# A hybrid attention and recurrence layer on one core: earlier weight splits, a two-pass rotary key, attention's output weights prepared one stage earlier, rotated queries written twice

## The chip, the core and the metric

The kernel runs on one core of a Trainium2 chip as one program. The metric is the device time of one execution in microseconds; smaller is better. The kernel before took 829.15 us (median of three runs, 826.8 to 831.96).

## What is computed

One layer over 1024 tokens of 1024 features, all in float32, cut to what matters here:

```python
h    = rms_norm(x, norm1_g) * (1 + scale1) + shift1      # mod = silu(c) @ w_ada + b_ada
proj = h @ w_in                  # 256 q latents, 128 kv latents, 64 rotary key, 512 x_lru, 512 g_lru
q    = rms_norm(q_lat) @ w_q_b   # 4 heads of 128 + 64 rotary
kv   = rms_norm(kv_lat) @ w_kv_b # 4 heads of 128 key + 128 value
attn = causal_softmax_attention(rope(q), rope(k), v)
lru  = scan(a, b) * gelu(g_lru)  # a, b from two sigmoid gates on a width-4 convolution of x_lru
mixed = concat([rms_norm(attn), rms_norm(lru)])          # 512 + 512
x    = x + gate1 * (mixed @ w_out)
h2   = rms_norm(x, norm2_g) * (1 + scale2) + shift2
x    = x + gate2 * experts(h2)   # 4 groups of 8 experts, top group, top 2 experts of it
```

## The kernel before

**Precision.** A float32 operand is cut into a high and a low part of a shorter format, and a product is made of three matmuls: high by high, high by low, low by high (`mm3`, L224 to L227). `split` (L216 to L222) makes the parts: a copy on ScalarE (ACT) writes the high part (L218, or L221 with a scale), and a subtraction writes the low one, on VectorE (DVE) or GpSimd (POOL) (L219, or L222 with a scale).

**Memory.** Most operands live in one pool of 41 blocks of 128 x 1024 floats (`blk`). A tile takes the block that is next in the ring, and waits until the readers of its last tenant are done. Transfers from memory stand in the queue of SyncE (SP): a load that waits for a block holds up the loads behind it. PSUM accumulators come from named banks: `pp` (projections) and `pL` (the recurrent branch's output) share three banks.

**Order.** The code is written as generators that are interleaved; a scheduler then fixes each engine's own instruction order at build time. Each engine runs its list strictly in order.

**Stages**, with the times of the trace:

- 0 to 180 us: twelve projections of the normalized input, one after the other in a list `FT`: kv latents, two of q latents, four of x_lru (`xl`), the rotary key (`kr`, index 7, 64 columns), and from index 8 four of g_lru (`gl0` to `gl3`). Between them stand the recurrence's gates (`gate_mm`, sigmoid; `gate`, exponentials, a square root L581, the scan L586) and the streamed modulation product (`wad`, L486 and L490). Projection i loads the weights of i+2 (`load_in`) and splits those of i+1 (`split_in`, L266).
- 180 to 233: the last gate, then `gl0` to `gl3` (`gl_steps`, L997) merged with head 0's keys and values (`pkv`). Each `gl` result goes through gelu, a product with the scan's output, and a square that POOL adds into `sqL` (L650).
- 233 to 246: head 0's queries (`pq`, L806). The rotary part of a pair of query tiles is formed by L521 to L524 on DVE and copied to a second place by POOL (L819).
- 246 to 297: `l_pass` (L1043), the recurrent branch's half of `mixed @ w_out`: 16 groups of 12 matmuls into `pL`, two groups to each of eight tiles of x (`xr`), which are stored back to `x_d`. Its weights come from `out_w([4, 5, 6, 7])` (L1017): four loads `wo`, 16 products with gate1 on POOL (L1027), and four scaled splits into `woh` and `wol` (L221, L222). The branch's norms (`pc`, L1040) need the finished `sqL`.
- 297 to 410: heads 0 to 2 (scores `pS`, probabilities `P`, transposed `PT`, values `po`), each merged with the preparation of the next one.
- 410 to 510: head 3 merged with attention's half of the output projection, whose weights come from `out_w([0, 1, 2, 3])`, stepped inside head 3.
- 510 to 545: router and lists; then to 825 the experts, with weights `ew` streamed by SP (L1101).

Of the kernel before, what the change touches and what calls it, by code (L numbers as in the profile page):

```python
# [22 lines left out]
NT = 8  # L23
# [115 lines left out]
def layer(ctx, tc, A, out, dbg=None, stop=None):  # L139
# [10 lines left out]
    def blk(name, dt=F32):  # L150
        return big.tile([128, 1024], dt, name=name, tag="b", bufs=NBLK)
# [64 lines left out]
    def split(src, hi, lo, scale=None, eng=None):  # L216
        if scale is None:
            SC.activation(hi, src, AF.Copy)  # L218
            (eng or V).tensor_sub(lo, src, hi)  # L219
        else:  # L220
            SC.activation(hi, src, AF.Copy, scale=scale)  # L221
            V.scalar_tensor_tensor(lo, src, scale, hi, op0=OP.mult, op1=OP.subtract)  # L222
# [6 lines left out]
    def t3(ap, t):  # L229
        return ap.rearrange("p (t f) -> p t f", t=t)  # L230
# [35 lines left out]
    def split_in(i):  # L266
        if i >= len(FT):
            return
        M = 64 if FT[i][0] == "kr" else 128
        w = wraw.pop(i)  # L270
        wh, wl = (t3(blk(n, F32R), 8)[:, :, :M] for n in ("winh", "winl"))
        split(w, wh, wl, eng=EN[OPT["in_lo" if i >= OPT["k1"] else "in_l1"]])
        wsp[i] = (wh, wl)

    pin = ctx.enter_context(ExitStack())
    pin.enter_context(ordered(*(EN[e] for e in OPT["pin"])))
# [247 lines left out]
        V.tensor_add(dst, dst, tmp)  # L524

    def project(i, n, ks=range(8)):
        M = 64 if FT[i][0] == "kr" else 128
        wh, wl = wsp[i]
        if 0 in ks:
            hold[i] = bank("pp")  # L530
        pp = hold[i]
        for k in ks:
            mm3(pp[:M], wh[:, k], wl[:, k], hTh[k][:, NS[n]], hTl[k][:, NS[n]], k == 0, k == 7)
            if k % 4 == 3:
                yield

# [87 lines left out]
    def k_rope(i, n):  # L624
        pp = hold.pop(i)
        if n == 0:
            lq["kr"] = blk("krT")
        kr = lq["kr"]
        SC.activation(kr[:64, NS[n]], pp[:64], AF.Copy)
        if n == 1:  # L630
            pk = bank("pk")
            for t in range(NT):
                T.transpose(pk[:, t * 64:(t + 1) * 64], kr[:64, t * 128:(t + 1) * 128], ident[:64, :64])
            kb = blk("kb")
            sqr, tmp = t3(kb[:, :512], NT), t3(kb[:, 512:], NT)
            SC.activation(sqr, t3(pk, NT), AF.Square)
            V.tensor_reduce(ssr, sqr, op=OP.add, axis=AX.X)
            rope(krr, t3(pk, NT), NT, "k", 0, tmp)

# [85 lines left out]
    for i in range(8):  # L725
        kind, j = FT[i]
        if i >= K1:
            load_in(i + 2)
            split_in(i + 1)
        if kind == "xl":  # L730
            load_gate(j)
        for n in range(2) if i >= K1 else (1,):
            for _ in project(i, n) if i >= K1 else ():
                for _ in range(OPT["adv"]):
                    next(ag, None)
            if n == (0 if i >= K1 else 1):
                gates()
            evac(i, n)
        if i < K1:
            wsp.pop(i)  # L740
        if i == 1:
            split_in(K1)
            V.tensor_scalar(rst, rsti, 0, None, op0=OP.is_equal)
            V.tensor_scalar(rcap, rst, -1.0, 2.0, op0=OP.mult, op1=OP.add)
        if kind == "xl":
            pend.append(j)
    wk = blk("wk")
    wq = [blk("wq")[:, :768] for _ in range(2)]
    SY.dma_start(wk, A["w_kv_b"])
    with tc.issue_after(last["x"]):  # L750
        for k in range(2):
            SY.dma_start(wq[k], A["w_q_b"][k * 128:(k + 1) * 128, :])
    gates(True)
    wkh, wkl = blk("wkh", F32R), blk("wkl", F32R)
    split(wk, wkh, wkl, eng=EN[OPT["wk_lo"]])
    drain(ag)
    sqL = blk("sqL")
    SCALE = 192.0 ** -0.5
# [3 lines left out]
    def prep(h, P):  # L762
# [39 lines left out]
        def q_mm(t0):  # L802
            pq = t3(bank("pq"), 2)[:, :, :192]
            for a in range(2):
                for k in range(2):
                    T.matmul(pq[:, a], latq[k][:, (t0 + a) * 128:(t0 + a) * 128 + 128], wq[k][:, h * 192:(h + 1) * 192],  # L806
                             start=(k == 0), stop=(k == 1))
            qnp = half("qnp").rearrange("p (c a d) -> p c a d", c=2, a=2)
            qn, qp = qnp[:, 0], qnp[:, 1]
            SC.activation(qn, pq[:, :, :128], AF.Copy)  # L810
            sqh = sm.tile([128, 2, 192], F32, name="sqh2", bufs=1)
            if OPT["ssh"]:
                for a in range(2):
                    SC.activation(sqh[:, a], pq[:, a], AF.Square, accum_out=ssh[:, t0 + a:t0 + a + 1])
            else:
                SC.activation(sqh, pq, AF.Square)
            tm = sm.tile([128, 2, 64], F32, name="qtmp", bufs=1)
            rope(qp[:, :, :64], pq[:, :, 128:], 2, "q", t0, tm)
            G.tensor_copy(qp[:, :, 64:], qp[:, :, :64])  # L819
            if not OPT["ssh"]:  # L820
                V.tensor_reduce(ssh[:, t0:t0 + 2], sqh, op=OP.add, axis=AX.X)
            qst[t0] = qn, qp
# [174 lines left out]
    def gl_steps():  # L997
        for i in range(8, 12):
            load_in(i + 2)
            split_in(i + 1)  # L1000
            for n in range(2):
                yield from project(i, n)
                evac(i, n)
                yield


# [36 lines left out]
    def l_pass():  # L1043
        mod_row("g1", 2)
        yield from out_w([4, 5, 6, 7])
        norms(ivL, sqL, list(range(NT)))
        for g in range(4):
            gs = slice(g * 256, g * 256 + 256)
            mh, ml = blk("mLh", F32R), blk("mLl", F32R)
            for j in range(4):  # L1050
                split(lru[j][:, gs], mh[:, j * 256:j * 256 + 256], ml[:, j * 256:j * 256 + 256], eng=EN[OPT["mL"]])
            for t in (2 * g, 2 * g + 1):
                x = blk("xr")
                SY.dma_start(x, A["x"][t * 128:(t + 1) * 128, :])
                for n in range(2):
                    pL = bank("pL")
                    for f in range(4):
                        c = slice(f * 256 + (t % 2) * 128, f * 256 + (t % 2) * 128 + 128)
                        mm3(pL, mh[:, c], ml[:, c], woh[4 + f][:, NS[n]], wol[4 + f][:, NS[n]], f == 0, f == 3)
                    V.scalar_tensor_tensor(x[:, NS[n]], pL, ivL[:, t:t + 1], x[:, NS[n]], op0=OP.mult, op1=OP.add)  # L1060
                    yield
                SY.dma_start(x1_d[t * 128:(t + 1) * 128, :], x)

# [75 lines left out]
    for h in range(3):  # L1139
# [1 line left out]
        ahead(30 + h)  # L1141
        merge((attention(h, P), OPT["mg"]), (prep(h + 1, Pn), NPREP))
        P = Pn
    ow = out_w([0, 1, 2, 3])
    next(ow)
    ahead(33)


# [239 lines left out]
    for i in attention(3, P, after):  # L1388
        if i is not None:
            ahead(20 + i)  # L1390
            next(ow, None)
            if i == OPT["rw"]:
                router_w()
            if i >= OPT["hk"]:
                next(ws_)
    drain(ow)
    if OPT["sep"]:
        phase(2)
    drain(ws_)
# [355 lines left out]
```

## Time and profile before

| what | value |
|---|---|
| median of three runs | 829.15 us (826.8 to 831.96) |
| the profiled execution | 831.86 us |
| its span in the trace | 830.1 us (1.76 us lie around it) |
| granted TensorE clock, mean | 0.956 |
| busy: PE / DVE / ACT / POOL | 736.3 / 449.1 / 316.9 / 163.5 us |

PE is TensorE's matmuls, PEld its weight loads, which overlap them. The profiled execution is 2.7 us above the median. A share of busy time is a mean over all stages; what a change is worth is read stage by stage: windows (busy time of each engine in a stretch), the timeline (instructions in order, with the idle time before each and what ended it) and the waits.

### The profile page before, as it was taken

To read this page: it belongs to the slowest core of one execution; us is meant where nothing else is said; L and a number is where in the kernel's file an instruction comes from. 1 tells how busy PE (TensorE), PEld (TensorE's weight loads), DVE (VectorE), ACT (ScalarE), POOL (GpSimd) and SP (SyncE) were. 2 spreads that over 40 slices of the span, in tenths; PEclk is the share of its full clock that TensorE was granted. 3 is DMA by queue.
4 is the path that set the end of the run, shared out by engine and by line. 5 is a ranking of instruction groups with operands and counts; after the bars stand their busy time and mean duration, and the time that the engine had idled before them with its cause. 6 is when DMAs were issued, how large, how long until landed. Compare 5 with 4: busy or idle time off the path is not lost. (4 is left out here: it accounts for less than half of the span.)

```text
span 830.1 us, 12292 instructions
## 1 busy us (share of the span) xinstructions
PE 736.3 (89%) x4265; PEld 475.6 (57%) x4265; DVE 449.1 (54%) x1332; ACT 316.9 (38%) x715; POOL 163.5 (20%) x167
## 2 busy tenths in 40 slices
PE   3799999996989989898979998599987799999985
PEld 1387766465878878788868887333333234333231
DVE  4597296886658359787985567343442122221311
ACT  3455555764444047667754444021111112120210
POOL 1111002122580002032631100111221111221101
PEclk9989999996989999999989999699988999999998
DMA  9942447681214340202144779999999999999993
GB/s 313 374 132 83 140 140 239 209 255 51 77 51 181 123 152 2 64 14 102 41 145 152 257 255 343 369 320 312 322 358 333 330 367 340 330 370 334 333 309 71
DMA packets 70976, 180.47 MB, mean 217 GB/s; under 512 B 8960, under 2 KB 22528, under 8 KB 70912
## 3 DMA queue, kind: packets, MB, share of 16 engines
q1 hardware_dynamic: 63328, 158.50, 53.9%
q0 software_dynamic: 7104, 21.00, 9.6%
q8 instruction: 34, 0.56, 0.3%
q10 hardware_dynamic: 480, 0.16, 0.2%
q14 instruction: 30, 0.25, 0.1%
HBM read 160.61 MB, written 22.95 MB: 221 GB/s over the span
## 5 line engine op out<-in xcount | busy, mean ns | idle before, releaser
L1629 PE MATMUL pgu<-ew,xeT 128*32 128x512 f32 (+1 forms) x928 | 165.3, 616 | 12.9 <-DMA ew<-in_w_e 11.6
L1629 PEld LDWEIGHTS pgu<-ew,xeT 128*32 128x32 f32 (+1 forms) x928 | 47.4, 122 | 104.6 <-issue 80.8
L225 PE MATMUL pp<-hTh,winh 128*128 128x512 f32 (+1 forms) x192 | 76.0, 408 | 5.1 <-DVE hTh L188 3.0
L1640 PE MATMUL py<-ew,hT 128*32 128x512 f32 (+1 forms) x464 | 78.4, 603 | 2.2 <-ACT hT L1614 2.2
L227 PE MATMUL pp<-hTh,winl 128*128 128x512 f32 (+1 forms) x192 | 77.2, 402 | 0.9 <-DVE winl L219 0.9
L226 PE MATMUL pp<-hTl,winh 128*128 128x512 f32 (+1 forms) x192 | 77.7, 405 | 0.0
L1643 DVE TENSOR_TENSOR y<-py,m_g 128x512 f32<-128x512 f32 (+1 forms) x40 | 27.7, 691 | 79.0 <-PE py L1640 74.2
L1603 ACT ACTIVATE sg<-pgu 128x256 f32<-128x256 f32 (+1 forms) x20 | 7.7, 387 | 133.0 <-PE pgu L1629 133.0
L1640 PEld LDWEIGHTS py<-ew,hT 128*32 128x32 f32 (+1 forms) x464 | 24.6, 121 | 47.1 <-issue 38.5
L1645 POOL DMA_INDIRECT out<-y,pki x13 | 20.7, 1596 | 134.2 <-DVE y L1643 118.3
L1596 DVE TENSOR_SCALAR xeT<-pxe,gc,mc 128x128 f32<-128x128 f32 x80 | 27.3, 403 | 35.1 <-PE pxe L1590 33.8
L225 PEld LDWEIGHTS pp<-hTh,winh 128*128 128x128 f32 (+1 forms) x192 | 36.5, 190 | 16.9 <-DVE hTh L188 3.9
L1614 ACT ACTIVATE hT<-pht 128x256 f32<-128x256 f32 (+1 forms) x20 | 7.6, 381 | 96.8 <-PE pht L1612 92.6
L1605 DVE SCALAR_TENSOR_TENSOR hid<-sg,pkw,pgu 128x256 f32<-128x256 f32 (+1 forms) x13 | 6.2, 478 | 69.4 <-ACT sg L1603 69.4
L227 PEld LDWEIGHTS pp<-hTh,winl 128*128 128x128 f32 (+1 forms) x192 | 36.2, 189 | 12.1 <-issue 2.5
L226 PEld LDWEIGHTS pp<-hTl,winh 128*128 128x128 f32 (+1 forms) x192 | 36.4, 189 | 11.6 <-issue 2.1
L1594 ACT ACTIVATE xeT<-pxe,mc,gc 128x128 f32<-128x128 f32 x80 | 30.0, 461 | 26.0 <-PE pxe L1590 26.0
L965 PE MATMUL po<-PT,v 128*128 128x256 f32 (+1 forms) x160 | 36.3, 366 | 0.0
L931 ACT ACTIVATE P<-pS,nb,scq 128x384 f32<-128x384 f32 (+2 forms) x48 | 32.4, 684 | 10.1 <-DVE nb L928 9.7
L965 PEld LDWEIGHTS po<-PT,v 128*128 128x128 f32 x160 | 29.3, 194 | 3.0
L806 PE MATMUL pq<-wq,latq 128*128 128x192 f32 x128 | 25.4, 352 | 5.7 <-DVE v L782 3.4
L1590 PEld LDWEIGHTS pxe<-ident,xe 128*128 128x128 f32 x160 | 18.5, 145 | 19.3 <-issue 12.3
(419 smaller groups left out, 1612.0 us busy)
## 6 DMA issues: line engine op xcount, KB each, us to landing
ew<-in_w_e SPq DMA_DIRECT2D x186, 512.0 KB
wad<-in_w_ada SPq DMA_DIRECT2D x64, 256.0 KB
wada<-in_w_ada SPq DMA_DIRECT2D x16, 512.0 KB
win<-in_w_in SPq DMA_DIRECT2D x12, 512.0 KB
xt<-in_x SPq DMA_DIRECT2D x8, 512.0 KB
wo<-in_w_out SPq DMA_DIRECT2D x8, 512.0 KB
xr<-in_x SPq DMA_DIRECT2D x8, 512.0 KB
x_d<-xr SPq DMA_DIRECT2D x8, 512.0 KB
```

The lines of the kernel that those rows point to most:

```text
L225: T.matmul(o, lhi, rhi, start=first, stop=False)
L226: T.matmul(o, lhi, rlo, start=False, stop=False)
L227: T.matmul(o, llo, rhi, start=False, stop=last)
L806: T.matmul(pq[:, a], latq[k][:, (t0 + a) * 128:(t0 + a) * 128 + 128], wq[k][:, h * 192:(h + 1) * 192], start=(k == 0), stop=(k == 1))
L931: SC.activation(Pt[:, o:o + w], pss[ci], AF.Exp, scale=P["scq"][:, i:i + 1], bias=nb, accum_out=l[:, ci:ci + 1])
L965: T.matmul(po[:, o:], P["v"][:, js], PT[j // 4][:, j % 4, o:], start=(j == 0), stop=(j == nj - 1), skip_group_check=True)
L1594: SC.activation(xT[a][:, c], pt[:, c], AF.Identity, scale=gc[:, k:k + 1], bias=sh2[:, k:k + 1])
L1596: last["dve"] = V.tensor_scalar(xT[a][:, c], pt[:, c], gc[:, k:k + 1], sh2[:, k:k + 1], op0=OP.mult, op1=OP.add).ins
L1629: T.matmul(pg[r], xT[k // 4][:, c + r.start:c + r.stop], w[k // 2][:, NS[k % 2]], start=(k == 0), stop=(k == 7), skip_group_check=True)
L1640: T.matmul(py[n][r], hT[:, a * 128 + r.start:a * 128 + r.stop], w[4 + a][:, NS[n]], start=(a == 0), stop=(a == 1), skip_group_check=True)
L1643: last["dve"] = V.tensor_mul(y[:rows, NS[n]], py[n][:rows], mrow["g2"][:rows, NS[n]]).ins
L1645: G.indirect_dma_start(out=out, out_offset=bass.IndirectOffsetOnAxis(ap=idx, axis=0), in_=y[r0:r0 + idx.shape[0]], in_offset=None, compute ...
```

## The change

Four edits. **One**: the rotary key's weights, high and low, stand in one block side by side (64 and 64 columns), so that two passes (against the high and the low input) give both parts in 128 rows instead of three passes with 64; the eight transposes that follow become eight matmuls against a stacked identity, which add the two halves. **Two**: the weights of `gl1` and of `w_kv_b` are split before the last gate, the latter's low part on DVE instead of POOL; each later `gl` is split two ahead, after the first half of a projection. **Three**: `out_w([0, 1, 2, 3])` is stepped inside `l_pass` instead of head 3: loads at its second quarter (`g == 1`), products and splits in the third and fourth. **Four**: the last addition of the rotated query writes both places, and POOL's copy goes.

```diff
--- before.py
+++ after.py
@@ -266,11 +266,15 @@
     def split_in(i):
         if i >= len(FT):
             return
-        M = 64 if FT[i][0] == "kr" else 128
         w = wraw.pop(i)
-        wh, wl = (t3(blk(n, F32R), 8)[:, :, :M] for n in ("winh", "winl"))
-        split(w, wh, wl, eng=EN[OPT["in_lo" if i >= OPT["k1"] else "in_l1"]])
-        wsp[i] = (wh, wl)
+        if FT[i][0] == "kr":
+            wb = t3(blk("winh", F32R), 8)
+            wh, wl = wb[:, :, :64], wb[:, :, 64:]
+            wsp[i] = (wb, None)
+        else:
+            wh, wl = wsp[i] = tuple(t3(blk(n, F32R), 8) for n in ("winh", "winl"))
+        last["hi"] = SC.activation(wh, w, AF.Copy).ins
+        last["lo"] = EN[OPT["in_lo" if i >= OPT["k1"] else "in_l1"]].tensor_sub(wl, w, wh).ins
 
     pin = ctx.enter_context(ExitStack())
     pin.enter_context(ordered(*(EN[e] for e in OPT["pin"])))
@@ -524,13 +528,16 @@
         V.tensor_add(dst, dst, tmp)
 
     def project(i, n, ks=range(8)):
-        M = 64 if FT[i][0] == "kr" else 128
         wh, wl = wsp[i]
         if 0 in ks:
             hold[i] = bank("pp")
         pp = hold[i]
         for k in ks:
-            mm3(pp[:M], wh[:, k], wl[:, k], hTh[k][:, NS[n]], hTl[k][:, NS[n]], k == 0, k == 7)
+            if wl is None:
+                T.matmul(pp, wh[:, k], hTh[k][:, NS[n]], start=(k == 0), stop=False)
+                T.matmul(pp, wh[:, k], hTl[k][:, NS[n]], start=False, stop=(k == 7))
+            else:
+                mm3(pp, wh[:, k], wl[:, k], hTh[k][:, NS[n]], hTl[k][:, NS[n]], k == 0, k == 7)
             if k % 4 == 3:
                 yield
 
@@ -626,14 +633,17 @@
         if n == 0:
             lq["kr"] = blk("krT")
         kr = lq["kr"]
-        SC.activation(kr[:64, NS[n]], pp[:64], AF.Copy)
+        SC.activation(kr[:, NS[n]], pp, AF.Copy)
         if n == 1:
+            i2 = half("ident2")[:, :64]
+            V.tensor_add(i2, ident[:, :64], ident[:, 64:])
             pk = bank("pk")
             for t in range(NT):
-                T.transpose(pk[:, t * 64:(t + 1) * 64], kr[:64, t * 128:(t + 1) * 128], ident[:64, :64])
+                T.matmul(pk[:, t * 64:(t + 1) * 64], kr[:, t * 128:(t + 1) * 128], i2, start=True, stop=True)
             kb = blk("kb")
             sqr, tmp = t3(kb[:, :512], NT), t3(kb[:, 512:], NT)
-            SC.activation(sqr, t3(pk, NT), AF.Square)
+            with tc.issue_after(last["hi"]):
+                SC.activation(sqr, t3(pk, NT), AF.Square)
             V.tensor_reduce(ssr, sqr, op=OP.add, axis=AX.X)
             rope(krr, t3(pk, NT), NT, "k", 0, tmp)
 
@@ -727,6 +737,8 @@
         if i >= K1:
             load_in(i + 2)
             split_in(i + 1)
+            if i == 7:
+                split_in(i + 2)
         if kind == "xl":
             load_gate(j)
         for n in range(2) if i >= K1 else (1,):
@@ -735,6 +747,12 @@
                     next(ag, None)
             if n == (0 if i >= K1 else 1):
                 gates()
+            if (i, n) == (7, 1):
+                wk = blk("wk")
+                SY.dma_start(wk, A["w_kv_b"])
+                wkh, wkl = blk("wkh", F32R), blk("wkl", F32R)
+                last["hi"] = SC.activation(wkh, wk, AF.Copy).ins
+                V.tensor_sub(wkl, wk, wkh)
             evac(i, n)
         if i < K1:
             wsp.pop(i)
@@ -744,15 +762,11 @@
             V.tensor_scalar(rcap, rst, -1.0, 2.0, op0=OP.mult, op1=OP.add)
         if kind == "xl":
             pend.append(j)
-    wk = blk("wk")
     wq = [blk("wq")[:, :768] for _ in range(2)]
-    SY.dma_start(wk, A["w_kv_b"])
     with tc.issue_after(last["x"]):
         for k in range(2):
             SY.dma_start(wq[k], A["w_q_b"][k * 128:(k + 1) * 128, :])
     gates(True)
-    wkh, wkl = blk("wkh", F32R), blk("wkl", F32R)
-    split(wk, wkh, wkl, eng=EN[OPT["wk_lo"]])
     drain(ag)
     sqL = blk("sqL")
     SCALE = 192.0 ** -0.5
@@ -815,8 +829,12 @@
             else:
                 SC.activation(sqh, pq, AF.Square)
             tm = sm.tile([128, 2, 64], F32, name="qtmp", bufs=1)
-            rope(qp[:, :, :64], pq[:, :, 128:], 2, "q", t0, tm)
-            G.tensor_copy(qp[:, :, 64:], qp[:, :, :64])
+            a_, b_ = tabs["q"]
+            V.tensor_mul(qp[:, :, 64:], pq[:, :, 128:], a_[:, t0:t0 + 2])
+            V.tensor_mul(tm[:, :, 0:32], pq[:, :, 160:], b_[:, t0:t0 + 2, 0:32])
+            V.tensor_mul(tm[:, :, 32:], pq[:, :, 128:160], b_[:, t0:t0 + 2, 32:])
+            two_ = lambda v: v[:, :, None, :].to_broadcast([128, 2, 2, 64])
+            V.tensor_add(qp.rearrange("p a (r d) -> p a r d", r=2), two_(qp[:, :, 64:]), two_(tm))
             if not OPT["ssh"]:
                 V.tensor_reduce(ssh[:, t0:t0 + 2], sqh, op=OP.add, axis=AX.X)
             qst[t0] = qn, qp
@@ -997,10 +1015,11 @@
     def gl_steps():
         for i in range(8, 12):
             load_in(i + 2)
-            split_in(i + 1)
             for n in range(2):
                 yield from project(i, n)
                 evac(i, n)
+                if n == 0:
+                    split_in(i + 2)
                 yield
 
 
@@ -1044,7 +1063,10 @@
         mod_row("g1", 2)
         yield from out_w([4, 5, 6, 7])
         norms(ivL, sqL, list(range(NT)))
+        ow = out_w([0, 1, 2, 3])
         for g in range(4):
+            if g == 1:
+                next(ow)
             gs = slice(g * 256, g * 256 + 256)
             mh, ml = blk("mLh", F32R), blk("mLl", F32R)
             for j in range(4):
@@ -1058,6 +1080,8 @@
                         c = slice(f * 256 + (t % 2) * 128, f * 256 + (t % 2) * 128 + 128)
                         mm3(pL, mh[:, c], ml[:, c], woh[4 + f][:, NS[n]], wol[4 + f][:, NS[n]], f == 0, f == 3)
                     V.scalar_tensor_tensor(x[:, NS[n]], pL, ivL[:, t:t + 1], x[:, NS[n]], op0=OP.mult, op1=OP.add)
+                    if g > 1:
+                        next(ow, None)
                     yield
                 SY.dma_start(x1_d[t * 128:(t + 1) * 128, :], x)
 
@@ -1141,8 +1165,6 @@
         ahead(30 + h)
         merge((attention(h, P), OPT["mg"]), (prep(h + 1, Pn), NPREP))
         P = Pn
-    ow = out_w([0, 1, 2, 3])
-    next(ow)
     ahead(33)
 
 
@@ -1388,12 +1410,10 @@
     for i in attention(3, P, after):
         if i is not None:
             ahead(20 + i)
-            next(ow, None)
             if i == OPT["rw"]:
                 router_w()
             if i >= OPT["hk"]:
                 next(ws_)
-    drain(ow)
     if OPT["sep"]:
         phase(2)
     drain(ws_)
```

**ACT at the last gate.** The rows are ACT's from the projection of the rotary key to the first gelu results; `winh` is the high part of a projection's weights, `wkh` that of `w_kv_b`, `kb` the square of the rotary key, `sqL` the square of the first gelu product; L581 (now L588) is the square root of a gate. Before:

```order
L218 ACTIVATE winh<-win 128x1024
L581 ACT_TABLE_LOAD
L581 ACTIVATE gt_wa<-gt_wa 128x1024
L564 ACT_TABLE_LOAD
...
L581 ACT_TABLE_LOAD
L581 ACTIVATE gt_wa<-gt_wa 128x1024
L636 ACTIVATE kb<-pk 128x512
L644 ACT_TABLE_LOAD
L644 ACTIVATE gelu<-pp 128x512 x2
L218 ACTIVATE wkh<-wk 128x1024
L218 ACTIVATE winh<-win 128x1024
L647 ACTIVATE sqL<-gt_wa 128x512 x2
```

With the change:

```order
L276 ACTIVATE winh<-win 128x1024 x2
L588 ACT_TABLE_LOAD
L588 ACTIVATE gt_wa<-gt_wa 128x1024
L571 ACT_TABLE_LOAD
...
L754 ACTIVATE wkh<-wk 128x1024
L588 ACT_TABLE_LOAD
L588 ACTIVATE gt_wa<-gt_wa 128x1024
L646 ACTIVATE kb<-pk 128x512
L654 ACT_TABLE_LOAD
L654 ACTIVATE gelu<-pp 128x512 x3
L657 ACTIVATE sqL<-gt_wa 128x512 x2
L276 ACTIVATE winh<-win 128x1024
```

The high part of `gl1` has moved ahead of the third gate's square root, `wkh` ahead of the last one's; the next high part (`gl2`) stands behind three gelus and two squares.

**POOL around the second output weights.** The rows are POOL's; `wo<-wo,m_g` is the product with gate1, four for each weight block, `sqA` belongs to head 3's results. Before, in head 2's end and head 3:

```order
L830 MEMSET ql 64x512
L1402 MEMSET xe 128x1024
L819 COPY qnp<-qnp 128x2x64
L976 TENSOR_TENSOR sqA<-sqA,sqa 128x256
L1027 TENSOR_TENSOR wo<-wo,m_g_1955 128x256 x16
L976 TENSOR_TENSOR sqA<-sqA,sqa 128x256 x4
```

With the change, in `l_pass`:

```order
L660 TENSOR_TENSOR sqL<-sqL,gelu 128x512
L848 MEMSET ql 64x512
L1046 TENSOR_TENSOR wo<-wo,m_g_1940 128x256 x16
L848 MEMSET ql 64x512
L807 TENSOR_TENSOR kraw<-kraw,ik 128x1024
L810 TENSOR_TENSOR sqh<-krr,ik 128x8x64 x2
```

The 16 products now stand ahead of the next head's key products (`kraw`, `sqh`), and no copy L819 is left.

**SP in l_pass.** The rows are SP's transfers, from the first output weights on. Before:

```order
L1021 DMA wo<-in_w_out 128x1024 x4
L1054 DMA xr<-in_x 128x1024 x2
L1062 DMA x_d<-xr 128x1024 x2
L1054 DMA xr<-in_x 128x1024 x6
L1062 DMA x_d<-xr 128x1024 x6
L1101 DMA ew<-in_w_e 128x1024 x7
L1021 DMA wo<-in_w_out 128x1024 x4
```

With the change:

```order
L1040 DMA wo<-in_w_out 128x1024 x4
L1076 DMA xr<-in_x 128x1024 x2
L1086 DMA x_d<-xr 128x1024
L1040 DMA wo<-in_w_out 128x1024
L1086 DMA x_d<-xr 128x1024
L1040 DMA wo<-in_w_out 128x1024 x3
L1076 DMA xr<-in_x 128x1024 x4
L1086 DMA x_d<-xr 128x1024 x2
L1076 DMA xr<-in_x 128x1024 x2
```

The second four weight loads, seven rows behind the first ones in the list of before, now stand between the second tile of x and the third.

## Rows read from the trace of the kernel before

**Rows 1.** The page: the span in 40 slices, DMA engines' busy tenths and GB/s.

```profile
DMA  9942447681214340202144779999999999999993
GB/s 313 374 132 83 140 140 239 209 255 51 77 51 181 123 152 2 64 14 102 41 145 152 257 255 343 369 320 312 322 358 333 330 367 340 330 370 334 333 309 71
```

**Rows 2.** Windows: stretch, length, busy PE, PEld, DVE, ACT, POOL, clock, DMA, GB/s.

```profile
180.00:200.00 20.00, 12.87 (x52) 9.80 (x51) 17.81 (x20) 9.55 (x12) 8.12 (x7) 0.67 0.21 61
330.00:340.00 10.00, 8.38 (x58) 7.57 (x57) 6.34 (x23) 4.78 (x14) 0.00 (x0) 1.00 0.00 1
410.00:420.00 10.00, 5.36 (x31) 4.24 (x29) 9.83 (x17) 4.34 (x10) 10.00 (x12) 0.95 0.17 52
420.00:430.00 10.00, 9.22 (x51) 8.79 (x52) 8.09 (x17) 6.92 (x15) 1.76 (x3) 0.71 0.32 112
```

**Rows 3.** Waits of SP's queue: us in total, times, longest.

```profile
SPq L1101 <- DMA ew<-in_w_e: 185.5, 144, 4.5
```

**Rows 4.** Timeline of PE at the last gate: start, us, instruction, idle before and releaser.

```profile
185.39 0.71 PE L633 MATMUL pk<-ident,krT 64*128 64x64 f32 x8
190.13 0.79 PE L225 MATMUL pkv<-wkh,latkh 128*128 128x256 f32 x2 [4.03 <-ACT wkh L218]
191.08 0.80 PE L225 MATMUL pp<-hTh,winh 128*128 128x512 f32 x1 [0.15 <-ACT winh L218]
...
195.22 0.58 PE L226 MATMUL pkv<-wkl,latkh 128*128 128x256 f32 x1 [2.06 <-POOL wkl L219]
...
196.90 0.80 PE L227 MATMUL pp<-hTh,winl 128*128 128x512 f32 x1 [0.89 <-DVE winl L219]
...
200.48 0.45 PE L226 MATMUL pp<-hTl,winh 128*128 128x512 f32 x1
```

**Rows 5.** The same in the last projections: first and last of 93 matmuls.

```profile
211.84 0.40 PE L225 MATMUL pp<-hTh,winh 128*128 128x512 f32 x1
...
232.73 0.39 PE L227 MATMUL pp<-hTh,winl 128*128 128x512 f32 x1
```

**Rows 6.** Timelines of SP, PE and ACT ahead of the third gate.

```profile
163.08 0.43 SPq L254 DMA_DIRECT2D win<-in_w_in  x1
...
167.75 1.06 PE L490 MATMUL pm<-wad,cs 128*32 128x512 f32 x8 [1.16 <-DMA wad<-in_w_ada]
...
163.81 1.04 ACT L218 ACTIVATE winh<-win 128x1024 fp32r<-128x1024 f32 x1
```

**Rows 7.** Timeline of POOL from the third addition to `sqL` to the last.

```profile
218.96 1.29 POOL L650 TENSOR_TENSOR sqL<-sqL,gelu 128x512 f32<-128x512 f32 x1 [4.66 <-ACT gelu L649]
...
228.36 8.50 POOL L1027 TENSOR_TENSOR wo<-wo,m_g 128x256 f32<-128x256 f32 x10
...
243.68 1.43 POOL L650 TENSOR_TENSOR sqL<-sqL,gelu 128x512 f32<-128x512 f32 x1
```

**Rows 8.** Timeline of PE at the start of `l_pass`.

```profile
246.06 0.48 PE L225 MATMUL pL<-woh,mLh 128*128 128x512 f32 x1
```

**Rows 9.** Timeline of DVE in `l_pass`: one of nine, 2.72 us apart.

```profile
278.87 0.75 DVE L1060 SCALAR_TENSOR_TENSOR xr<-pL,ivL,xr 128x512 f32<-128x512 f32 x1 [1.97 <-PE pL L227]
```

**Rows 10.** Timeline of POOL in head 3; durations of line L222 (min/median/max ns).

```profile
407.01 13.34 POOL L1027 TENSOR_TENSOR wo<-wo,m_g 128x256 f32<-128x256 f32 x16
...
L222 DVE SCALAR_TENSOR_TENSOR wol<-wo,col,woh x8: 1273/1285/2247, 224.2 to 424.6; 128x1024 fp32r<-128x1024 f32 x8
```

**Rows 11.** Timeline of DVE: the same scaling during POOL's products, and in head 0.

```profile
411.79 0.87 DVE L945 TENSOR_SCALAR P<-P,rl 128x128 f32<-128x128 f32 x1
...
300.60 0.28 DVE L945 TENSOR_SCALAR P<-P,rl 128x128 f32<-128x128 f32 x1
```

**Rows 12.** Durations of two lines on DVE (min/median/max ns).

```profile
L524 DVE TENSOR_TENSOR qnp<-qnp,qtmp x16: 275/292/855, 240.2 to 402.8; 128x128 f32<-128x128 f32 x16
...
L219 DVE TENSOR_TENSOR mLl<-gt_wa,mLh x16: 405/417/1481, 243.5 to 266.0; 128x256 fp32r<-128x256 f32 x16
```

**Rows 13.** Waits from 300 to 420 us: us in total, times, longest.

```profile
PE ptP L952 <- ACT P L931: 2.5, 2, 1.6
```

## The prediction

> **What bounds the kernel now.** I read the page's slices first, then windows by stage, then the timelines at the holes. Two regimes show. From about 540 us on the DMA engines are busy nine tenths or more of every slice but the last, at 309 to 370 GB/s [rows 1], and SP waited 144 times, 185.5 us in all, for an earlier load of expert weights [rows 3]: there the stream of weights sets the pace. Its loads wait for blocks that the stages ahead give back, so the stream begins earlier when those stages end earlier. Before that TensorE is the limiter wherever it is full, and time is lost only where it is not. In the windows [rows 2] it is idle 7.1 of 20 us at 180 to 200, at a granted clock of 0.67; 4.6 of 10 us at 410 to 420; and at 420 to 430 it is busy 9.22 us at a clock of 0.71. An ordinary head (330 to 340) has 8.38 of 10 at full clock. The change touches the first two of these places and puts work into l_pass, which is nearly full. So the sum is three stretches of PE's timeline, and every microsecond saved ahead of 430 is taken to move all that follows.
>
> **Part two, the last gate.** PE's transposes end at 186.10 (185.39 + 0.71), and at 200.48 it is back at full pace [rows 4]. In these 14.4 us it does 12 matmuls of 512 columns and 4 of 256. At full clock 93 of the long ones took 232.73 − 211.84 = 20.89 us, 0.227 us apiece [rows 5]; a short one half of it. The work is worth 12 × 0.227 + 4 × 0.114 = 3.2 us, so 11.2 us are lost: 4.03 us waiting for wkh, 2.06 for wkl, 0.89 for the low part of gl0 [rows 4], the rest on half a clock (0.67 in the window, with matmuls 0.43 us apart between 197.5 and 200.1) after these stalls. All three operands are now made earlier: wkh ahead of the last gate's square root, wkl on DVE, both parts of gl1 before the gate. What is late next? First, ACT's queue: gl1's high part (1.04 us [rows 6]) now stands ahead of the third gate's square root, and it needs the load issued at 163.08, which shares the DMA engines with modulation pieces, for which PE waited until 167.75 [rows 6]. I estimate that load to land at 168 to 169.5, against 164.85 when ACT ended the high part ahead (163.81 + 1.04), so the gates' chain on ACT and DVE slips 3 to 4.5 us. Second, gl2's high part now stands behind three gelus and two squares, which wait for the scan; PE has 24 matmuls of gl1 (5.4 us) and head 0's pkv to cover that, and runs dry for 1 to 3 us. Bounds: 11.2 if nothing is late, 3.7 if both slips land whole on PE (11.2 − 4.5 − 3). I take 8, in the upper half since the matmuls of gl0 and gl1 are there to run while the gate finishes.
>
> **Part one, the rotary key.** 48 matmuls become 32: 16 × 0.227 = 3.6 us of PE [rows 5]. Matmuls on 64 and on 128 columns of weights move 512 columns either way, so the price is the count. The unmoved waits of that stretch (convolution output for the gates, the modulation piece at 167.75 [rows 6]) give part of it back: between 0 and 3.6 I take 1.5, below half, because the next event there is a load. The eight plain matmuls in place of transposes (0.71 us for all eight [rows 4]) and one addition on DVE: under 1 us either way, hidden beside the scan, at nothing; without that cover it is 1 us.
>
> **The chain to l_pass.** POOL is busy without a break from the third addition to sqL at 218.96 to the end of the last at 243.68 + 1.43 = 245.11, and the first pL matmul is at 246.06 [rows 7, 8]: ten products alone take 8.50 us. This chain starts on a gelu result, so it moves with parts one and two; two copies leave it (0.3 to 0.9 us each by the DVE twin of their size [rows 12]; at least 0.6): +0.5. l_pass then starts 8 + 1.5 + 0.5 = 10 us earlier, at 236 (bounds 3.7 and 11.2 + 3.6 + 0.5 = 15.3).
>
> **Part three, what it puts into l_pass.** 16 products on POOL, 13.34 us in head 3 [rows 10]; four scaled low parts on DVE, 1.285 us each [rows 10], 5.1 in all, with as many high parts on ACT; four loads of 512 KB. POOL and ACT have little to do there. DVE takes 0.75 us of each 2.72 us group and idles 1.97 [rows 9]: over 16 groups 31 us are free, so 5.1 fit, with the products' own disturbance too. Queued behind: three weight loads now stand ahead of the third tile of x in SP's list. 1.57 MB at 374 GB/s, the page's best slice [rows 1], are 4.2 us. The tile's reader is the addition that frees a pL bank; three banks are two groups ahead, so that some of the 4.2 us is covered. PE waits 0 (all covered) to 4.2 us; a gain is excluded, since nothing leaves this stage but copies. I take 1.5.
>
> The same edit in head 3: at 410 to 430 PE lost 4.64 us by idling, then 0.78 and 9.22 × 0.29 = 2.67 by the clock: 8.1 us [rows 2]. An ordinary head loses 1.62 in 10, 3.2 in 20. Gain 8.1 − 3.2 = 4.9, taken as 5; bounds 3 (the router's weights and head 3's start remain in DVE's list) and 8.1. Here a scaling of 128 x 128 took DVE 0.87 us beside POOL's products against 0.28 in head 0 [rows 11], so these products slow DVE, and through it the softmax, well beyond their own count.
>
> The Trainium skill, "SBUF — State Buffer", section "SBUF: two separate sides", says that DVE and GpSimd take turns on one shared port pair, held for a whole instruction, the loser blocked. By that rule the 13.34 us would stop DVE wherever they stand, l_pass included; by the rows there is room for them, and the sum keeps 1.5 us.
>
> **Part four.** The second copy makes DVE's addition 256 wide: 0.417 against 0.292 us [rows 12], 16 × 0.125 = 2.0 us over four heads, beside PE's work; 16 POOL copies and a hop DVE to POOL go. Taken at nothing; without the cover −2.0, and up to +1 at head 0's queries.
>
> **Sum.** 10 − 1.5 + 5 = 13.5 us. The profiled execution took 831.86 (span 830.1 and 1.76 around it): 818.4 for it. It stands 2.7 above the median 829.15, so the prediction is 829.15 − 13.5 = 815.65. All bad ends at once give 3.7 − 4.2 + 3 − 2 = 0.5, all good ones 15.3 + 8.1 + 1 = 24.4; without either pile-up the forecast's own range is a gain of 6 to 22, 807 to 823.
>
> **Rivals.**
> - *The hole only moves.* ACT stands before the third gate's square root for gl1's load, the gate ends so late that gl2 waits, and POOL's chain sets l_pass. For: the load stands among modulation pieces that PE itself waits for [rows 6]. Against: 11.2 us were lost to operands that are now early. Front gain 2: 829.15 − 2 + 1.5 − 5 = 823.7.
> - *The products' price is paid again in l_pass.* DVE, blocked 13.34 us, delays the additions that free pL; two spare groups (5.4 us) cover part, 8 us remain: 829.15 − 10 − 5 + 8 = 822. It is the shared-port rule named above, at work on this kernel. Against: DVE idles 1.97 of 2.72 us [rows 9].
> - *The stream of weights ends the kernel anyway.* 144 waits on it [rows 3]; if its start did not follow the stages ahead, 829. Against: the middle slices of the page move 2 to 181 GB/s [rows 1], so it is blocks, not the DMA engines, that hold it.
> - *Slower: blocks run out in the heads.* woh and wol of attention, eight of 41 blocks, are now held through heads 0 to 2, whose P and PT take blocks row by row; each then waits for an older reader. A late P costs PE 2.5 / 2 = 1.25 us [rows 13]; 24 rows give 30 us: 829.15 − 13.5 + 30 = 845.7. It decides from 13.5 / 24 = 0.56 us a row. Against: in the built order every block that P or PT takes had its last reader at least 80 instructions earlier (109 before).
> - *More.* All 11.2, 3.6 and 8.1 come in: 829.15 − 11.2 − 3.6 − 0.5 − 8.1 = 805.8.
>
> **Numbers.** Forecast 0.62, the hole moves 0.10, l_pass pays 0.06, the stream 0.06, slower 0.09, more 0.07. About 1% (8.3 us) is what a measurement tells from no change. Faster by over 1% (below 820.9): 0.56 of the forecast, the last case's 0.07, and 0.04 of the lower ends of the 822 and 823.7 cases: 0.67. Slower: 0.09. Within 1%: 0.24. From 804 to 826 lie the forecast, the first two rivals and more than half of the last; the stream, slower and the rest of the last are left out, 0.18.
>
> **What would show it.** Right: PE at 186 to 200 without the 4 us wait for wkh and at 0.227 us a matmul; the first pL about 236; 16 products inside l_pass with PE above 9.5 in 10; the start of head 3 at 8 or more in 10; expert loads shifted by the same amount. Wrong: ACT idle on the load of win ahead of the third square root; PE in l_pass waiting for xr's addition; P or PT waiting on a block in heads 0 to 2; an expert stage longer by what was saved ahead.

## The result, and the profile after

The changed kernel took 816.39 us (median of four runs, 814.67 to 817.67) against 828.78 beside it: a ratio of 0.985 (95% interval 0.982 to 0.988), 12.4 us less. In a later comparison it took 815.59 against 829.10, a ratio of 0.983 (0.981 to 0.986), 13.5 us less. The forecast was 815.65, 13.5 less. Its profiled execution took 816.14 us.

Four points of PE's timeline split the gain: the first and the last matmul of l_pass (`pL`), the first of attention's output projection (`pA`, the start of its last part inside head 3), and the expert stage's first transposes (`pxe`). Starts in us:

| kernel | pL first | pL last | pA first | pxe first | l_pass | heads (pL last to pA) |
|---|---|---|---|---|---|---|
| before | 246.1 | 294.8 | 438.2 | 531.5 | 48.7 | 143.4 |
| changed | 235.3 | 286.3 | 423.8 | 517.0 | 51.0 | 137.5 |
| gain | 10.8 | 8.5 | 14.4 | 14.5 | −2.3 | 5.9 |

So 10.8 us come from the front, l_pass pays 2.3, the heads give 5.9, and nothing is lost up to the experts. The table's rows, from the durations of the matmuls by tile (min/median/max ns, first and last start), of the kernel before:

```profile
L225 PE MATMUL pL<-woh,mLh x64: 387/389/496, 246.1 to 294.3; 128*128 128x512 f32 x64
L227 PE MATMUL pL<-woh,mLl x64: 387/389/486, 247.7 to 294.8; 128*128 128x512 f32 x64
L225 PE MATMUL pA<-woh,mAh x64: 389/389/498, 438.2 to 508.6; 128*128 128x512 f32 x64
```

and of the changed one:

```profile
L225 PE MATMUL pL<-woh,mLh x64: 387/389/504, 235.3 to 285.9; 128*128 128x512 f32 x64
L227 PE MATMUL pL<-woh,mLl x64: 388/389/481, 237.6 to 286.3; 128*128 128x512 f32 x64
L225 PE MATMUL pA<-woh,mAh x64: 389/389/498, 423.8 to 494.2; 128*128 128x512 f32 x64
L1610 PE MATMUL pxe<-ident,xe x160: 272/273/476, 517.0 to 776.5; 128*128 128x128 f32 x160
```

Windows of the changed kernel (columns as in [rows 2]): the last gate, head 3's start, and l_pass.

```profile
186.00:206.00 20.00, 20.00 (x109) 17.23 (x108) 17.64 (x30) 11.46 (x20) 4.02 (x4) 1.00 0.37 121
405.00:425.00 20.00, 19.16 (x123) 16.70 (x122) 17.61 (x55) 13.32 (x35) 2.62 (x3) 1.00 0.50 169
...
250.00:260.00 10.00, 9.25 (x44) 7.52 (x45) 6.75 (x16) 6.14 (x14) 5.95 (x8) 1.00 1.00 363
260.00:270.00 10.00, 8.84 (x41) 7.15 (x40) 8.41 (x12) 4.02 (x7) 6.85 (x8) 1.00 0.54 202
```

Both holes of [rows 2] are closed, at full clock; a shallow one has opened in l_pass. PE's timeline at the last gate, against [rows 4]:

```profile
174.65 0.50 PE L225 MATMUL pg<-xch,gws 128*128 128x512 f32 x1 [1.05 <-ACT gt_wa L571]
...
179.34 0.50 PE L225 MATMUL pp<-hTh,winh 128*128 128x512 f32 x1 [0.84 <-ACT krT L636]
...
188.58 0.28 PE L225 MATMUL pkv<-wkh,latkh 128*128 128x256 f32 x1
188.69 0.28 PE L226 MATMUL pkv<-wkl,latkh 128*128 128x256 f32 x1
188.81 1.90 PE L642 MATMUL pk<-ident,krT 128*128 128x64 f32 x16
```

The waits for wkh and wkl are gone. What is late instead stands on ACT, against [rows 6]:

```profile
169.16 1.06 ACT L276 ACTIVATE winh<-win 128x1024 fp32r<-128x1024 f32 x1 [4.90 <-DMA win<-in_w_in]
...
171.53 1.06 ACT L588 ACTIVATE gt_wa<-gt_wa 128x1024 f32<-128x1024 f32 x1
```

POOL's products: eight of the sixteen of the first weights, all of which run ahead of l_pass, and twelve of the sixteen of the second, all of which run in it (against [rows 7, 10]):

```profile
211.42 5.60 POOL L1046 TENSOR_TENSOR wo<-wo,m_g 128x256 f32<-128x256 f32 x8
...
254.92 11.40 POOL L1046 TENSOR_TENSOR wo<-wo,m_g 128x256 f32<-128x256 f32 x12 [4.05 <-DMA wo<-in_w_out]
```

DVE's list in l_pass, then PE's two waits there that the kernel before did not have:

```profile
255.69 1.75 DVE L222 SCALAR_TENSOR_TENSOR wol<-wo,col,woh 128x1024 fp32r<-128x1024 f32 x1 [0.19 <-ACT woh L221]
259.96 1.28 DVE L222 SCALAR_TENSOR_TENSOR wol<-wo,col,woh 128x1024 fp32r<-128x1024 f32 x1 [2.52 <-ACT woh L221]
261.16 1.40 DVE L1082 SCALAR_TENSOR_TENSOR xr<-pL,ivL,xr 128x512 f32<-128x512 f32 x2
```

```profile
250.18 0.44 PE L851 MATMUL ptq<-ident,qnp 128*128 128x128 f32 x2 [0.98 <-DVE ks L870]
...
261.96 0.50 PE L225 MATMUL pL<-woh,mLh 128*128 128x512 f32 x1 [1.16 <-DVE xr L1082]
```

The first wait comes from PE's own list: these transposes of head 0's queries now stand ahead of the second quarter's first matmul (251.41), where u3 below, which differs by part three alone, has them behind it. The second comes from DVE's list: two low parts stand ahead of the third tile's additions; they wait for ACT, ACT for POOL's products, and those for the loads. PE then waits for the addition.

### The profile page after: what moved, and what is told of

It is laid out like the page before. It is cut to its first block, busy times and chain, and to the rows that moved or that the text cites. A ratio compares the mean times of both kernels' runs of the same rounds, so it can differ in the third digit from the quotient of the medians.

```text
span 814.4 us, 12262 instructions
## 1 busy us (share of the span) xinstructions
PE 730.2 (90%) x4257; PEld 470.3 (58%) x4257; DVE 447.6 (55%) x1334; ACT 317.3 (39%) x715; POOL 157.6 (19%) x150
## 5 line engine op out<-in xcount | busy, mean ns | idle before, releaser
L225 PE MATMUL pp<-hTh,winh 128*128 128x512 f32 x176 | 68.2, 400 | 5.8 <-DVE hTh L188 3.0
L226 PE MATMUL pp<-hTl,winh 128*128 128x512 f32 x176 | 70.1, 398 | 0.2 <-DVE hTl L469 0.2
L227 PE MATMUL pp<-hTh,winl 128*128 128x512 f32 x176 | 69.5, 396 | 0.0
L225 PEld LDWEIGHTS pp<-hTh,winh 128*128 128x128 f32 x176 | 33.4, 190 | 16.2 <-DVE hTh L188 4.0
L226 PEld LDWEIGHTS pp<-hTl,winh 128*128 128x128 f32 x176 | 33.4, 190 | 9.9 <-issue 2.1
L227 PEld LDWEIGHTS pp<-hTh,winl 128*128 128x128 f32 x176 | 33.4, 190 | 8.3 <-DVE lq L587 0.8
L1046 POOL TENSOR_TENSOR wo<-wo,m_g 128x256 f32<-128x256 f32 x32 | 28.2, 917 | 15.5 <-DMA wo<-in_w_out 15.5
## 6 DMA issues: line engine op xcount, KB each, us to landing
wada<-in_w_ada SPq DMA_DIRECT2D x16, 512.0 KB, 10.8
```

The lines of the kernel that those rows point to most:

```text
L225: T.matmul(o, lhi, rhi, start=first, stop=False)
L226: T.matmul(o, lhi, rlo, start=False, stop=False)
L227: T.matmul(o, llo, rhi, start=False, stop=last)
L1046: EN[OPT["g1"]].tensor_mul(w[:, q:q + 256], w[:, q:q + 256], mrow["g1"][:, q:q + 256])
```

## Experiments: one part undone, or one part alone

The milestones ahead of the experts repeat within 0.1 us for the length of a stage (heads 137.5 and 137.4, l_pass 51.0 and 50.9 in two profiles of the changed kernel) and 0.7 us for a point (pxe 517.0, 517.7). With the same code up to there a point can differ by more: pL starts at 234.3 to 235.9 in the changed kernel, c1, u3, m1 and m4, and at 246.1 and 247.8 in the kernel before and m3, so 1.7 us or less at one point tell nothing by themselves. From pxe to the end it took 291 to 299 us with unchanged expert code, so parts are told apart by the milestones, and totals by runs.

**The changed kernel again (c1).** 

> The changed kernel again, as a base on this chip: 814 to 818 us, the first pL matmul at 235.3, the first expert transposes (pxe) at 517.

 Measured: 815.59 us; pL 235.9, pxe 517.7. The total is as expected, the points 0.6 and 0.7 us later.

**Part one undone (u1).** `project`, `k_rope` and `split_in` as before for `kr`:

```diff
...
-                T.matmul(pp, wh[:, k], hTh[k][:, NS[n]], start=(k == 0), stop=False)
-                T.matmul(pp, wh[:, k], hTl[k][:, NS[n]], start=False, stop=(k == 7))
...
+            mm3(pp[:M], wh[:, k], wl[:, k], hTh[k][:, NS[n]], hTl[k][:, NS[n]], k == 0, k == 7)
```

> The changed kernel with the rotary key back in three passes and transposes (part one undone). Theory: the key's projection now ends earlier (161.3 against 163.2 us), but ScalarE then stands 4.9 us before the load of gl1's weights, so the two saved microseconds are waited away: undoing costs 0 to 0.5 us. Rival, the prediction's sum: 1.5 us slower.

 Measured: 817.04 us, ratio 0.986 (0.984 to 0.989); pL at 235.0, pxe at 517.8. The theory holds: the key's 3.6 us of PE are worth nothing at pL. ACT's timeline shows why: gl1's high part waits for its load with three passes too, and starts 0.25 us after the changed kernel's (169.16), as does the gate's next matmul on PE (174.89 against 174.65):

```profile
169.41 1.06 ACT L272 ACTIVATE winh<-win 128x1024 fp32r<-128x1024 f32 x1 [4.45 <-DMA win<-in_w_in]
...
174.89 0.50 PE L225 MATMUL pg<-xch,gws 128*128 128x512 f32 x1 [2.58 <-ACT gt_wa L564]
```

The totals alone would not decide between 0.5 and 1.5 us.

**Part two undone (u2).**

```diff
-            if i == 7:
-                split_in(i + 2)
...
-            if (i, n) == (7, 1):
-                wk = blk("wk")
...
+    split(wk, wkh, wkl, eng=EN[OPT["wk_lo"]])
```

> The changed kernel with the splits of gl1 and w_kv_b back behind the last gate (part two undone). Theory, the prediction's step: PE stalls for wkh, wkl and the low part and runs at half clock again, 8 to 9 us slower, the first pL matmul about 8 us later. Rival (the hole only moved, the gain came from the shorter key and the shorter POOL chain): 0 to 3 us slower.

 Measured: 827.8 us, ratio 0.998 (0.996 to 1.000), 11.4 above the changed kernel; pL at 249.9, pA at 438.1. The old waits are back, one of them longer, in PE's timeline:

```profile
191.36 0.80 PE L225 MATMUL pkv<-wkh,latkh 128*128 128x256 f32 x2 [4.03 <-ACT wkh L218]
198.93 0.80 PE L227 MATMUL pp<-hTh,winl 128*128 128x512 f32 x1 [4.54 <-DVE winl L277]
```

14.6 us at pL, more than the theory's 8: without the early splits the other parts make the front worse by 3.8 (249.9 against 246.1, or by 2.1 against m3's 247.8), with DVE's low part of gl0 4.54 us late instead of 0.89.

**Part two alone (c2).** The kernel before with the lines put in that u2 takes out. 

> The kernel before with part two alone (early splits of gl1 and w_kv_b). Theory: nearly the whole gain ahead of l_pass is part two's, first pL at 235 to 236.5 against 246.1, and head 3's hole stays: 819 to 821 us. Rival (the parts need each other): first pL at 238 or later.

 Measured: 819.22 us, ratio 0.988 (0.985 to 0.992); pL at 235.6, from there as slow in the heads as before (144.0 us). The theory holds: part two alone brings 10.5 of the front's 10.8 us.

**Part three undone (u3).** `out_w([0, 1, 2, 3])` stepped in head 3 again:

```diff
-        ow = out_w([0, 1, 2, 3])
...
-            if g == 1:
-                next(ow)
...
-                    if g > 1:
-                        next(ow, None)
...
+            next(ow, None)
```

> The changed kernel with attention's output weights prepared in head 3 again (part three undone). Theory: the 8 us hole at the start of head 3 comes back and l_pass gets 2 us shorter, 6 us slower in all. Rival (l_pass pays the whole price too): within 1 us.

 Measured: 822.25 us, ratio 0.994 (0.991 to 0.996), 5.9 above the changed kernel. l_pass takes 48.4 us (235.3 to 283.7), so part three costs it 2.6; the heads take 147.9, 10.4 more than with the early weights.

**Part four undone (u4).** `rope` and POOL's copy again:

```diff
...
-            V.tensor_add(qp.rearrange("p a (r d) -> p a r d", r=2), two_(qp[:, :, 64:]), two_(tm))
+            rope(qp[:, :, :64], pq[:, :, 128:], 2, "q", t0, tm)
+            G.tensor_copy(qp[:, :, 64:], qp[:, :, :64])
```

> The changed kernel with the 16 copies of rotated queries back on POOL (part four undone). Theory: in heads 0 to 2 the changed kernel lost 0.7 us a head, about as much as four 256-wide additions on DVE cost more than 128-wide ones (0.5 us), so DVE is on the path there, and undoing makes it about 2 us faster. Rival, the prediction's step: within 0.5 us of the changed kernel, or up to 1 us slower by the hop to POOL.

 Measured: 812.21 us, ratio 0.981 (0.978 to 0.984), about 4 us below the changed kernel. The theory holds in its place: the heads take 135.3 us (pL last 287.4, pA 422.7) instead of 137.5:

```profile
L225 PE MATMUL pL<-woh,mLh x64: 387/389/628, 234.6 to 286.9; 128*128 128x512 f32 x64
L227 PE MATMUL pL<-woh,mLl x64: 387/389/774, 236.1 to 287.4; 128*128 128x512 f32 x64
L225 PE MATMUL pA<-woh,mAh x64: 389/389/497, 422.7 to 493.2; 128*128 128x512 f32 x64
```

l_pass was 1.8 us longer there (52.8 us), behind a wait of 2.03 us at 250.85 and with a granted clock of 0.82 and 0.84 from 250 to 255 and from 255 to 260 (1.00 in the changed kernel, and in all of l_pass in c4 below, which has the same copies). So pxe (516.1) stood only 0.9 earlier; the rest of the 4 us lies in the expert stage, which this edit does not touch.

## Experiments on single suspects

**Loads behind the fourth tile of x (m1).**

```diff
-            if g == 1:
-                next(ow)
...
+                if t == 3:
+                    next(ow)
```

> The changed kernel with the four loads of attention's output weights issued after the fourth tile of x instead of ahead of the third. In the changed kernel VectorE's list has two scaled subtractions ahead of the third tile's first addition, and they waited for these loads; l_pass took 51.0 us from first to last pL matmul against 48.7 before. Theory: with the additions first, l_pass is back at 48.7 to 49.2 us, about 2 us faster. Rival (the price is the products on GpSimd beside VectorE): l_pass stays at 51 us.

 Measured: 815.44 us, ratio 0.984 (0.981 to 0.986); l_pass 49.4 us, pxe 515.5. DVE's list now has the third tile's additions first, PE's has the transposes behind the second quarter's first matmul again, and the waits of 1.16 and 0.98 us are gone; one of 0.61 us for DVE's `mLl` has come at 274.30. Of the 2.6 us that part three costs in l_pass, 1.6 were this order, though the products stayed beside DVE. That is just short of the theory's 48.7 to 49.2. In the totals 1 us is not told from none.

**Products left out in the kernel before (m3)** and **in the changed one (m4)**, the same edit:

```diff
-            for q in range(0, D, 256):
+            for q in range(0, D, 256) if f > 3 else ():
```

Without gate1 the tokens go to other experts, so nothing after head 3 is compared. 

> The kernel before without the 16 products of attention's output weights with gate1 on GpSimd (left out: gate1 on attention's half); loads and splits stay in head 3. Theory (the products stop VectorE, and the splits wait for them): from the last pL to the first pA matmul it takes 137 to 138 us, as in the changed kernel, instead of 143.4. Rival (the splits in the lists of ScalarE and VectorE are the price): above 141 us.

 Measured: heads 141.4 us (296.4 to 437.8). The theory was wrong: the products are 2.0 of the hole's microseconds. Yet they do slow DVE, as two rows show at the place of [rows 11] (0.87 us there) and of the low part, which took in the kernel before:

```profile
412.62 1.74 DVE L222 SCALAR_TENSOR_TENSOR wol<-wo,col,woh 128x1024 fp32r<-128x1024 f32 x1
```

and in m3:

```profile
412.44 0.29 DVE L945 TENSOR_SCALAR P<-P,rl 128x128 f32<-128x128 f32 x1
413.26 1.28 DVE L222 SCALAR_TENSOR_TENSOR wol<-wo,col,woh 128x1024 fp32r<-128x1024 f32 x1 [0.53 <-ACT woh L221]
```

> The changed kernel without the same 16 products (left out: gate1 on attention's half), which now stood in l_pass. Theory (loads ahead of the tiles of x are the price): l_pass stays at 50 to 51 us, since the subtractions still wait for the loads. Rival (the rule of one port pair, products beside VectorE): back at 48.7 us.

 Measured: l_pass 49.6 us (234.3 to 283.9), between theory and rival. The wait of 0.98 us is still there and the one of 1.16 is gone: the chain was load, products, high part, low part, addition, and taking the products out shortens it. In the changed kernel one product of that chain (256.32 us) took 1.73 us beside a low part, where the one after it, beside none, took 0.73. I estimate from these durations that about 1.0 of the 1.16 us is POOL and DVE in each other's way; no run takes that apart from the chain. Once the order is right, u3 leaves at most 1.0 us for the products beside DVE (49.4 in m1 against 48.4).

**gl1's load earlier (m2).**

```diff
-            load_in(i + 2)
+            if i < 7:
+                load_in(i + 2)
+            if i == 6:
+                load_in(9)
```

> The changed kernel with gl1's load issued together with gl0's, ahead of eight modulation pieces (139.5 instead of 162.5 us). Theory: ScalarE's wait of 4.90 us for this load goes, the third gate ends as much earlier, and of PE's waits ahead of gl1 (1.46, 1.05, 0.84 us) the last two go: first pL matmul at 233 to 234 instead of 235.3. Rival (POOL's chain or the moved modulation pieces set the end): first pL within 0.5 us of 235.3, or later.

 Measured: 811.74 us, ratio 0.980 (0.976 to 0.985); pL at 233.3, pxe at 515.0. The wait on ACT is gone, and both high parts run together:

```profile
163.11 1.99 ACT L276 ACTIVATE winh<-win 128x1024 fp32r<-128x1024 f32 x2
...
166.99 1.06 ACT L588 ACTIVATE gt_wa<-gt_wa 128x1024 f32<-128x1024 f32 x1
```

The third square root starts 4.5 us earlier and pL 2.0, as the theory has it. But in this profile PE ran at a granted clock of 0.72 from 160 to 170 us, where the changed kernel has 1.00, so 2.0 need not be the whole worth of the early load (c3 has more).

**Both (c3).** The edits of m1 and m2. 

> The changed kernel with gl1's load issued early and attention's output weights loaded behind the fourth tile of x, both at once. By the two traces alone: first pL 2.0 us earlier, l_pass 1.6 us shorter, pxe at 513.4, 3.6 us faster than the changed kernel. Rival (the stream of expert weights sets the end): the first expert step comes earlier, but the end by less than 2 us.

 Measured: 809.68 us, ratio 0.977 (0.973 to 0.980); pL 230.9, l_pass 50.4 (235 matmuls between its ends, where m1 has 227), pxe 512.1, 5.6 us before c1's. More than the sum expected, by a pL 2.4 us earlier than m2's. By the last of the gates' matmuls c3 is already 2.3 us ahead (173.2 against 175.5), and what differs up to there is the granted clock, as the windows of m2 and of c3 show (the last three columns are clock, DMA and GB/s):

```profile
160.00:170.00 10.00, 7.60 (x29) 2.80 (x28) 9.86 (x15) 7.97 (x9) 0.00 (x0) 0.72 0.62 210
...
160.00:170.00 10.00, 7.05 (x33) 3.38 (x34) 9.90 (x14) 7.64 (x9) 0.01 (x1) 1.00 0.74 239
```

Why the clock fell in m2 and not in c3 stays open; c3's PE was the less busy one in that stretch (7.05 us against 7.60).

**And POOL's copies (c4).** 

> The same with the rotated queries' copies back on GpSimd (part four undone). Theory: one more microsecond earlier at pxe (the trace with copies alone had 516.1 against 517.0) and within 1 us of the kernel without copies in all; the 4 us that the copies alone showed came from the stream of expert weights, which is not theirs. Rival: 3 to 4 us faster again.

 Measured: 809.02 us, ratio 0.976 (0.974 to 0.978); heads 135.2 us against c3's 137.4, pL 1.0 later (no more than a point differs by itself), pxe 1.0 earlier (511.1). The theory holds. c3 and c4 beat both kernels, by some 20 us the one before and 6 the changed one; between them the runs do not decide.

## Why the prediction was right, and where its terms were not

Two of the four signs that the prediction named for being wrong did show: ACT idle on the load of win (4.90 us), and PE in l_pass waiting for an addition to xr (1.16 us). Both turned out to be costs that the sum had counted, not its failure.

**The bound** held: what was saved ahead of 430 us arrived. In all eleven profiles of kernels with the full computation, the gain at pxe and the gain of the median over the kernel before agree within 2.3 us, from 0.1 and 1.4 (u2) to 20.4 and 20.1 (c4). SP's long row of expert loads began 14.5 us earlier, and it waited about as much for the stream itself as in [rows 3]; before, then changed:

```profile
516.53 23.38 SPq L1101 DMA_DIRECT2D ew<-in_w_e  x13
...
502.05 35.50 SPq L1125 DMA_DIRECT2D ew<-in_w_e  x19
...
SPq L1125 <- DMA ew<-in_w_e: 188.8, 152, 4.8
```

The rival that the stream sets the end is out.

**The last gate**, taken as 8 us, is worth 10.5 alone (c2). The first of the two slips came as described (ACT, 4.90 us before gl1's load) and costs 2.0 us at pL by m2 and 4.4 by c3 (230.9 against 235.3 in m1), so the runs leave the 3 to 4.5 of the prediction standing. The second did not show: PE is busy 20.00 of 20 us from 186 to 206.

**The rotary key**, taken as 1.5 us, is worth none (u1). The step's own reason, waits that do not move, took it: gl1's load holds the gates, whenever the key is done. The eight plain matmuls took 1.90 us where the transposes took 0.71 [rows 4], 1.2 more and not "under 1 us". What the shorter key is worth with that load early, no run shows. The 0.5 us for the copies that leave POOL's chain shows nowhere: with the copies back pL starts at 234.6 (u4), no later than without. So 8 + 1.5 + 0.5 came near 10.8 by errors of opposite sign, which is luck.

**l_pass**, taken as −1.5, is −2.6 (u3), inside its bounds. The forecast's path, a tile of x landing late, was not it. About half is a changed order in PE's own list (the wait of 0.98 us, there with and without products). The other half (1.16 us) does come from the loads, by low parts put ahead of the additions in DVE's list, waiting for those loads and the products on them. That DVE has room on average [rows 9] said nothing on the order of its list. The room itself was also less than the 31 us computed from those groups: over the whole of l_pass (246.1 to 294.8) DVE was busy 25.43 of 48.70 us, which leaves 23.

**Head 3**, taken as 5 us, gave 8.2: 143.4 us before against 135.2 in c4, which has the same copies and no such step in head 3. All of it falls into head 3: its first scores start 112.1 us after the last pL matmul in both. From there to the first pA, before and in c4 (columns as in [rows 2]):

```profile
406.90:438.20 31.30, 25.79 (x152) 22.72 (x150) 28.21 (x72) 18.69 (x41) 15.94 (x20) 0.89 0.31 103
...
394.60:417.70 23.10, 22.98 (x152) 20.44 (x150) 19.84 (x68) 14.59 (x37) 2.82 (x4) 1.00 0.42 140
```

The same 152 matmuls lost 5.5 us to idle time and now lose 0.1; the other 2.8 us are the lower clock. So it is the whole of the 8.1 us computed as lost: the step that failed is the 3.2 us taken off as an ordinary head's idle time, which head 3 does not have. Of the 8.2 the products are 2.0 (m3); the other 6.2 lie with the loads, the splits and their order, which no run takes apart.

**Part four**, taken as nothing, cost 2.2 us: every kernel here with the wide additions and early weights has 137.4 or 137.5 us in the heads (changed, c1, c3, u1, u2, m1, m2, m4), the two with copies and early weights 135.2 and 135.3. The named price without cover (2.0) is near it, but it was not paid evenly over four heads: head 3's first scores start 112.9 us after the last pL with the wide additions and 112.1 with copies, so 0.8 is lost in three heads and 1.4 in head 3. 8.2 − 2.2 make the 5.9 measured (to rounding), near the 5 of the sum, by two more errors of opposite sign. The two parts are not independent: beside the wide additions the step in head 3 costs 10.4 (u3), and with that step in head 3 the wide additions cost 3.9 (u3 against c2).

**The Trainium skill**, "SBUF — State Buffer", section "SBUF: two separate sides", has the two engines block each other where DVE's instruction runs in a two-port mode or reads two operands from SBUF. The prediction took it to hold wherever they meet. In head 3 the trace agrees that DVE is held up beside POOL's products (0.87 against 0.29 us with and without them). In l_pass three products took 1.73 to 1.74 us instead of 0.73 to 0.75, each beside a low part, which reads two operands from SBUF. The additions there, with one operand from PSUM, take their 0.75 us beside the products, and the rival built on the rule (8 us paid again) did not come. PE's busy share in l_pass, forecast above 9.5 in 10, fell to 9.25 and 8.84, by the two waits named above.

**Blocks** in the heads: 137.4 us with the eight blocks held from l_pass on, and 135.2 with copies; nothing of the 30 us feared. Up to head 3's first scores c4 takes the 112.1 us of the kernel before, so holding them costs the heads nothing that shows.

## What to carry to other kernels

An operand that a full TensorE waits for after a long serial step is best prepared before that step, but then the next thing late is the load of that operand: look where it stands among other transfers. The average room of an engine does not tell whether work fits; its list in order does, and one instruction that waits for a load holds up all behind it. When a sum of terms comes out right, undo the parts one by one before believing the terms: here each was off, and they cancelled.

## Not expected of the hardware

GpSimd's products were not slower beside a busy VectorE as such. Of the twelve from 254.92 us on, nine took 0.73 to 0.75 us and three 1.73 to 1.74, and each of the three began while a low part `wol` ran on VectorE. The eight from 211.42 us on took 5.60 us, 0.70 each, though VectorE was busy 5.36 of the 5.60 us from 211.40 to 217.00; there it was VectorE's steps of 128x8 that were long, 0.66 us against 0.16 or 0.17 at 241.4, without products. And the expert stage with unchanged code took 291 to 299 us from profile to profile, in no relation to what was edited. Runs of one kernel differ as much (c3: 804.96 to 814.24), so much of it is from run to run; what moves it stays open.
